# Stick-breaking attention in a two-layer decoder trunk: value products of two units placed together, projections dealt three and one per step

## The chip, the cores and the metric

The kernel runs on one core of a Trainium2 chip. The metric is the device time of one execution in microseconds; before the change the median of three runs is 2117.93 us (2116.54 to 2119.25). The engines are named as in the profile: PE multiplies matrices (PEld loads its weights, beside it), DVE is the vector engine, ACT the scalar engine, POOL the general one, and SP issues most transfers. Each engine runs its own instructions strictly in the order in which they were written, and waits on semaphores for the others.

## The reference

The model has two layers, 1024 tokens and a width of 1024, all in float32. Layer 0 is a gated linear recurrence, layer 1 stick-breaking attention with 16 heads of 64; each is followed by a SwiGLU network, and an RMS norm stands before each part and at the end. The change touches the attention alone:

```python
def stick_breaking_attention(x, w_qkv, w_o):
    qkv = jnp.einsum("bsd,de->bse", x, w_qkv).reshape(bsz, seq, 3, N_HEADS, HEAD_DIM)
    ...
    for blk in range(seq // Q_BLOCK):
        ...
        z = jnp.einsum("bhqd,bhkd->bhqk", qb, kb).astype(jnp.float32) * scale
        ...
        log_fail = jnp.where(strict, jax.nn.log_sigmoid(-z), 0.0)
        suffix = lax.cumsum(log_fail, axis=3, reverse=True) - log_fail
        weights = jnp.where(strict, jnp.exp(jax.nn.log_sigmoid(z) + suffix), 0.0)
        outs.append(jnp.einsum("bhqk,bhkd->bhqd", weights.astype(vb.dtype), vb))
```

The kernel writes the weights as differences of running products of sigmoid(-z), taken from the right. So a row of scores needs one sigmoid and one multiplying scan, and the products are taken with differences of neighbouring values (`VV`).

## The kernel before, in words

The attention stage is one loop over steps u, from -10 to 191 (line 1915), with the order of every engine written out by hand: what is written first runs first on its engine. 16 heads in 8 pairs q give 192 chunks of scores and 192 units of products, 12 of each per head, so a pair takes 24 steps. Step u does:

- the scores of chunk u + 10: two float32 matmuls into one of two PSUM buffers `z_ps` (`z_part`, lines 1690 and 1691); ACT takes their sigmoid into `w` (`z_rest`, line 1728), which frees the buffer, and DVE scans `w` (`scan`, lines 1735 and 1738);
- for the chunk of the step before, ACT casts `w` to float16 and DVE takes the remainder (`turn_weights`, lines 1750 and 1751), and a transfer on SP transposes both (line 1760);
- the products of unit u: two to four float16 matmuls into `av_ps` (`av_part`, line 1802). An even unit has them after the scan, an odd one at the end of the step. Units 3 and 11 of a head close their output bank, which ACT and DVE then gather (`oo`, lines 1814 and 1815), and POOL adds the values (line 1819);
- one task of the queue `later` (weights, norms, gathering), and at the start of the step all tasks that were staged for it (`stage` and `due`);
- from u = -2 on, two calls of the generator of projections (`fill`).

The generator (`qkv_steps`, line 1571) makes queries, keys and values of the next pair (`which` 0, 1 and 2), each in two halves n of 512 tokens. A half is eight groups of three float32 matmuls into `qk_ps` (lines 143 to 145), and each call gives one group. The eighth group ends a half and begins its eviction; the next call ends the eviction and gives the first group of the next half:

```python
                        if i < ND - 1:
                            yield
                    ev = evacuate(q, which, n, ps)
                    next(ev)
                    yield
                    next(ev, None)
```

Of an eviction (`evacuate`, line 1600) the first part reads PSUM: for queries ACT's cast `two<-qk_ps` (L1660), for keys DVE's multiplication `two<-qk_ps,rbc` (L1665), for values DVE's `vt<-qk_ps` (L1610). The second part does, for queries, DVE's low part (L1651) and stages the copies to the heads (L1648). For keys it stages ACT's cast `two<-two` (L1673) for the next step; this stages the low part (L1651) and the first two key copies (L1640) for the step after, and these the last two copies. For values it takes the difference (L1612) and stages its cast (L1627).

When the generator turns to the keys it also puts the three parts of the next weights (L1558 and L1559) and of the column norms into `later`: two squares on ACT (`sq<-raw`, L1553) and the sums on PE (`n_ps<-g,sq`, L1537). The sums take a `z_ps` buffer in turn with the scores.

For the last pair (from u = 166) the weights are transposed on PE instead (`t_part`, `t_split`, lines 1770, 1779 and 1780), two units at an even step; the generator has ended by then, and some groups of the output projection (`out_work`) fill in.

Of the kernel before, what the change touches and what calls it, by code (L numbers as in the profile page):

```python
# [34 lines left out]
def trunk(  # L35
# [166 lines left out]
    def stats(acc, ps_pool, tag, n, i0=0, i1=4):  # L202
        ps = ps_pool.tile([P, NB], F32, tag=tag, name="st_ps")
        accs = acc if isinstance(acc, tuple) else (acc,)
        for i in range(i0, i1):
            for a in accs:
                nc.tensor.matmul(
                    ps[:, i : i + 1], lhsT=a[:, i * P : (i + 1) * P], rhs=ones, start=a is accs[0], stop=a is accs[-1]
                )
        rstd(rcol[:, 4 * n + i0 : 4 * n + i1], ps[:, i0:i1])  # L210
# [1277 lines left out]
    with ExitStack() as st:  # L1488
# [31 lines left out]
        def stage(task, steps=1):  # L1520
            soon.append([steps, task])

        def load_link(i):
            q, which = divmod(i, 3)
            if q < NP:
                raws[i] = load_raw(cols(w_qkv, which * D + q * P), (ND,))
            else:
                mix[0].load(which)
# [233 lines left out]
        def unit_list(q, hx):  # L1762
            kbs = ((0, 1, 2, 3), (4, 5, 6, 7, 0, 1, 2, 3))
            return [(q, hx, G, kb, kb == 4 * G, kb == 3) for G in range(2) for kb in kbs[G]]

        def t_part(q, hx, G, kb, first, last):
            tp = psT.tile([P, NB], F32, tag="T", name="wt_ps")
            for j in range(max(kb, 4 * G), 4 * G + 4):
                c = (j - 4 * G) * P
                nc.tensor.transpose(  # L1770
                    tp[:, c : c + P], W[q, hx, j, kb // 4][:, (kb % 4) * P : (kb % 4 + 1) * P], ident
                )
            return tp
# [11 lines left out]
        def av_part(q, hx, G, kb, first, last):  # L1785
            q0 = (max(kb, 4 * G) - 4 * G) * P
            if first:
                av[0] = psO.tile([P, NB], F32, tag="o", name="av_ps")
            ps = av[0]
            k = kb % 4  # L1790
            parts_ = []
            if q == LAST:
                parts_ = [(q0, NB, t[:, q0:].rearrange("p (j c) -> p j c", c=P)) for t in ready.pop((hx, G, kb))]
            else:
                T_ = T[q, hx, G, kb // 4 == G]
                if kb // 4 == G and k < 2:
                    tp = T[q, hx, G, "pair"]
                    parts_ = [(q0, 2 * P, tp[:, x : x + 3 : 2] if k == 0 else tp[:, 4 + x : 5 + x]) for x in range(2)]
                c0 = max(q0, 2 * P) if kb // 4 == G else 0
                parts_ += [(c0, NB, T_[:, 2 * k + x, max(k - 2, 0) * (kb // 4 == G) :]) for x in range(2)]  # L1800
            for i, (c0, c1, t) in enumerate(parts_):
                nc.tensor.matmul(  # L1802
                    ps[:, c0:c1].rearrange("p (j c) -> p j c", c=P), lhsT=VV[q][:, hx, kb], rhs=t,
                    start=first and i == 0, stop=last and i == len(parts_) - 1,
                )
            if not last:
                return
            a, b = (top, bot)[:: 1 if hx == 0 else -1]

            def gather():  # L1810
                if hx == 0:
                    oo[q, G] = ap.tile([P, NB], F32, tag="oo", name="oo", bufs=2)
                o = oo[q, G]
                nc.scalar.copy(o[a], ps[b])
                nc.vector.tensor_add(o[a], ps[a], o[a])

            def add_v():
                eng = nc.vector if q == NP - 1 else nc.gpsimd
                eng.tensor_add(oo[q, G], oo[q, G], VT[q][:, G * NB + 1 : (G + 1) * NB + 1])

            def parts():
                o = oo[q, G]
                down = f32(av_[q])

                def both(hi, lo):
                    nc.scalar.activation(hi, o, AF.Copy, scale=down)
                    nc.vector.scalar_tensor_tensor(lo, o, down, f32(hi), op0=ALU.mult, op1=ALU.subtract)

                if not kept(q, G):
                    both(xh[q][G], xl[q][G])  # L1830
                else:
                    oh = ap.tile([P, NB], F32R, tag="oh", name="oh", bufs=1)
                    both(oh, o.bitcast(F32R))

                    def store():
                        nc.sync.dma_start(od[q, G][0], f32(oh))
                        nc.sync.dma_start(od[q, G][1], o)

                    stage(store)

            later.insert(0, gather)
            if hx == 1:
                later.extend((add_v, lambda: None, parts))
# [3 lines left out]
        units = [u for q, hx in heads for u in unit_list(q, hx)]  # L1847
# [27 lines left out]
        with tc.manual_schedule(engines={E.PE, E.Activation, E.DVE, E.Pool, E.SP}):  # L1875


            load_link(1)
            first = qkv_steps(0)
            between = {  # L1880
                12: lambda: stats(rbc[0], psO, "o", 0),
                16: lambda: stats(rbc[1], psO, "o", 1),
                17: lambda: broadcast_r(psO, "o", 0),
                18: lambda: nc.gpsimd.tensor_scalar_mul(rs, rcol, -SC),
                21: lambda: broadcast_r(psO, "o", 1),
            }
            def due():
                now = soon[:]
                soon.clear()
                for steps, task in now:  # L1890
                    if steps > 1:
                        stage(task, steps - 1)
                    else:
                        task()

            for i in range(1, 2 * ND * NH + 3 + AHEAD):
                next(first)
                if i in between:
                    between[i]()
                due()  # L1900
                if i > 4 and later:
                    later.pop(0)()

            gains = [len(units) - x for x in (31, 29, 27)]

            last_two, out_work = len(units) - 2 * 12, out_fill()
            amount = {x: 2 for x in (9, 10, 11, 12)}
            amount.update({x: 1 for x in (*range(-5, 1), *range(14, 21))})
            c = 0

            def turn(some):
                for a in some:
                    turn_weights(*a)

            for u in range(-LEAD, len(units)):
                some = chunks[c : c + 1]
                c += 1
                if u < -2:
                    for _ in range(2):
                        next(fill, None)  # L1920
                due()
                for _ in range(2 if u >= last_two - 8 and u % 2 == 0 else 1):
                    if back:
                        nc.sync.dma_start(*back.pop(0))
                for a in some:
                    z_rest(z_part(*a), *a)
                if u % 2 == 0 and u + 2 >= last_two:
                    av_part(*units[u])
                    two = [(x, t_part(*x)) for x in units[u + 2 : u + 4]]
                    for x, tp in two:  # L1930
                        ready[x[1:4]] = t_split(tp, *x)
                for a in some:
                    scan(*a)
                now, turning = turning, list(some)
                turn(now)
                if u % 2 == 0 and 0 <= u < last_two - 2:
                    av_part(*units[u])
                if u - last_two == 9:
                    mix[0].w[mix[0].order[1]] = next_weights(mix[0].raw.pop(1), nc.gpsimd)
                if later:  # L1940
                    later.pop(0)()
                if u >= -2:
                    for _ in range(2):
                        next(fill, None)
                for _ in range(amount.get(u - last_two, 0)):
                    next(out_work)
                if u in gains:
                    z_rest(z_part(*chunks[c]), *chunks[c])
                    scan(*chunks[c])
                    turning.append(chunks[c])  # L1950
                    c += 1
                if u % 2 and u >= 0:
                    av_part(*units[u])
            while later or soon:
                due()
                if later:
                    later.pop(0)()
# [46 lines left out]
```

## Time and profile before

| | us |
|---|---|
| median of three runs | 2117.93 |
| the profiled execution | 2116.7 |
| its span | 2114.9 |
| attention loop within the span, about | 985 to 1400 |
| PE busy | 2096.8 |
| DVE busy | 1771.3 |
| ACT busy | 1184.5 |

The span runs from the first to the last instruction; 1.8 us of the profiled execution lie outside it. Times of rows are counted from the start of the span. Matmuls are pipelined: a row's length is longer than the distance to the next row's start, and this distance is what a matmul costs. In the order of time a row has start, length, engine, line, operation, written<-read tiles and shape; idle time of the engine ahead of it stands in brackets with what ended it, and xN merges N in a row. In the list of waits a row has who waited for whom, total us, times, and the longest.

### The profile page before, as it was taken

How to read it: one execution, taken by the hardware profiler on the slowest of the kernel's cores; microseconds unless marked ns; L12 is line 12 of the kernel's file. 1: busy time of each engine (PE TensorE's matmuls, PEld its weight loads, DVE VectorE, ACT ScalarE, POOL GpSimd, SP SyncE). 2: the span in 40 equal slices, each digit the busy share in tenths (PEclk: the TensorE clock that was granted, in tenths of full speed). 3: DMA queues.
4: the chain of work that ended last, by engine and by line, in shares of the span. 5: the costliest groups of instructions: out<-in, count | busy, mean ns of one | idle time of the engine just before them, and what ended most of it. 6: DMA issues, size and time to landing. Idle time of an engine off the chain costs nothing.

```text
span 2114.9 us, 27976 instructions
## 1 busy us (share of the span) xinstructions
PE 2096.8 (99%) x10022; PEld 1719.9 (81%) x10022; DVE 1771.3 (84%) x2579; ACT 1184.5 (56%) x1906; POOL 139.1 (7%) x118
## 2 busy tenths in 40 slices
PE   8999999999999999999999999999999999999998
PEld 7888888888888888887777777678888888888887
DVE  7888778888888788796999999967888888888886
ACT  6567535444344445466878878744544444454456
POOL 1222010000000000000011111012000000000002
PEclk9999999999999999999999999999999999999999
DMA  7111431334444776533888898942224444686452
GB/s 240 50 50 40 149 100 55 105 124 145 161 133 152 256 251 190 152 118 91 162 179 175 177 178 174 247 170 80 85 90 150 140 150 155 202 269 225 126 153 90
DMA packets 446444, 313.89 MB, mean 148 GB/s; under 512 B 166104, under 2 KB 361824, under 8 KB 446304
## 3 DMA queue, kind: packets, MB, share of 16 engines
q1 hardware_dynamic: 446144, 311.84, 51.1%
q8 instruction: 78, 1.28, 0.3%
q14 instruction: 62, 0.51, 0.1%
q10 hardware_dynamic: 160, 0.27, 0.0%
HBM read 183.57 MB, written 82.84 MB: 126 GB/s over the span
## 4 chain that ended last, share of the span: by engine, by line
PE 93%; DVE 3%; ACT 1%; DMA 1%; issue 1%; SPq 0%; DVEq 0%; ACTq 0%
PE p_ps L143 18%; PE p_ps L145 18%; PE p_ps L144 18%; PE qk_ps L143 3%; PE qk_ps L145 3%; PE qk_ps L144 3%; PE a_ps L144 3%; PE a_ps L145 3%; PE a_ps L143 3%; PE ob_ps L143 3%; PE ob_ps L145 3%; PE ob_ps L144 3%; PE av_ps L1802 2%; PE i_ps L145 1%; PE i_ps L144 1%; PE i_ps L143 1%
## 5 line engine op out<-in xcount | busy, mean ns | idle before, releaser
L143 PE MATMUL p_ps<-vh,wbh 128*128 128x512 f32 x524 | 204.9, 391 | 0.0
L144 PE MATMUL p_ps<-vl,wbh 128*128 128x512 f32 x524 | 204.5, 390 | 0.0
L145 PE MATMUL p_ps<-vh,wbl 128*128 128x512 f32 x524 | 204.0, 389 | 0.2 <-DVE wbl L726 0.2
L143 PE MATMUL p_ps<-vh,wch 128*128 128x512 f32 x524 | 204.2, 390 | 0.0
L145 PE MATMUL p_ps<-vh,wcl 128*128 128x512 f32 x524 | 204.1, 389 | 0.0
L144 PE MATMUL p_ps<-vl,wch 128*128 128x512 f32 x524 | 203.9, 389 | 0.0
L722 ACT CAST wbh<-sb 128x1024 fp32r<-128x1024 f32 (+2 forms) x69 | 69.6, 1009 | 192.6 <-DVE sb L702 192.6
L145 PE MATMUL p_ps<-vh,wal 128*128 128x512 f32 x396 | 154.0, 389 | 0.0
L143 PE MATMUL p_ps<-vh,wah 128*128 128x512 f32 x396 | 154.0, 389 | 0.0
L144 PE MATMUL p_ps<-vl,wah 128*128 128x512 f32 x396 | 154.0, 389 | 0.0
L145 PEld LDWEIGHTS p_ps<-vh,wbl 128*128 128x128 f32 x524 | 98.4, 188 | 21.6 <-DVE wbl L726 0.7
L145 PEld LDWEIGHTS p_ps<-vh,wcl 128*128 128x128 f32 x524 | 98.4, 188 | 20.9 <-DVE wcl L736 0.6
L143 PEld LDWEIGHTS p_ps<-vh,wch 128*128 128x128 f32 x524 | 98.4, 188 | 20.5 <-ACT tb L1181 0.2
L144 PEld LDWEIGHTS p_ps<-vl,wch 128*128 128x128 f32 x524 | 98.3, 188 | 20.5
L143 PEld LDWEIGHTS p_ps<-vh,wbh 128*128 128x128 f32 x524 | 98.6, 188 | 19.8 <-ACT U L1181 0.4
L144 PEld LDWEIGHTS p_ps<-vl,wbh 128*128 128x128 f32 x524 | 98.6, 188 | 18.5
L143 PE MATMUL qk_ps<-vh,whi 128*128 128x512 f32 x264 | 113.2, 429 | 0.0
L1728 ACT ACTIVATE w<-z_ps,rs 128x512 f32<-128x512 f32 (+2 forms) x168 | 96.7, 579 | 15.1 <-PE z_ps L1691 12.0
L144 PE MATMUL qk_ps<-vl,whi 128*128 128x512 f32 x264 | 103.8, 393 | 0.0
L145 PE MATMUL qk_ps<-vh,wlo 128*128 128x512 f32 x264 | 103.7, 393 | 0.0
L1750 ACT CAST wx<-w 128x512 f16<-128x512 f32 (+1 forms) x140 | 80.1, 572 | 38.4 <-DVE w L1735 20.0
L1735 DVE TENSOR_TENSOR_SCAN w<-w,unit 128x128 f32<-128x128 f32 (+1 forms) x112 | 93.4, 834 | 9.5 <-ACT w L1728 8.3
(417 smaller groups left out, 5834.3 us busy)
## 6 DMA issues: line engine op xcount, KB each, us to landing
raw<-in_ffn_w_in SPq DMA_DIRECT2D x88, 512.0 KB, 4.0
vl<-pd SPq DMA_DIRECT2D x128, 256.0 KB, 3.6
pd<-U SPq DMA_DIRECT2D x90, 256.0 KB, 2.3
raw<-in_ffn_w_out SPq DMA_DIRECT2D x56, 256.0 KB, 3.6
raw<-in_attn_w_qkv SPq DMA_DIRECT2D x24, 512.0 KB, 4.2
h<-hd SPq DMA_DIRECT2D x32, 256.0 KB, 5.7
hd<-h SPq DMA_DIRECT2D x32, 256.0 KB, 2.0
g<-hd SPq DMA_DIRECT2D x32, 256.0 KB, 5.3
```

The costliest lines, as they stand in the source:

```text
L143: nc.tensor.matmul(ps, lhsT=wh, rhs=mh, start=first, stop=False, **kw)
L144: nc.tensor.matmul(ps, lhsT=wh, rhs=ml, start=False, stop=False, **kw)
L145: nc.tensor.matmul(ps, lhsT=wl, rhs=mh, start=False, stop=last, **kw)
L722: nc.scalar.copy(self.full(self.wb), self.full(self.sb))
L1728: nc.scalar.activation(F, ps[:, 0:n], AF.Sigmoid, scale=rs[:, j : j + 1])
L1735: nc.vector.tensor_tensor_scan(rev, rev, unit[:, NB - n :][:, ::-1], 0.0, op0=ALU.mult, op1=ALU.add)
L1750: nc.scalar.copy(wx[:, 0:m, 0], F)
L1802: nc.tensor.matmul(ps[:, c0:c1].rearrange("p (j c) -> p j c", c=P), lhsT=VV[q][:, hx, kb], rhs=t, start=first and i == 0, stop=last and i ...
```

## The change

Two things. The products of an even unit leave their place in the even step, in the main part and in the last pair alike, and stand at the end of the odd step, right ahead of those of the odd unit. And the generator is called three times in an even step and once in an odd one, instead of twice in each. The number of calls, of instructions and of transfers stays the same.

```diff
@@ -1925,7 +1925,6 @@
                 for a in some:
                     z_rest(z_part(*a), *a)
                 if u % 2 == 0 and u + 2 >= last_two:
-                    av_part(*units[u])
                     two = [(x, t_part(*x)) for x in units[u + 2 : u + 4]]
                     for x, tp in two:
                         ready[x[1:4]] = t_split(tp, *x)
@@ -1933,14 +1932,12 @@
                     scan(*a)
                 now, turning = turning, list(some)
                 turn(now)
-                if u % 2 == 0 and 0 <= u < last_two - 2:
-                    av_part(*units[u])
                 if u - last_two == 9:
                     mix[0].w[mix[0].order[1]] = next_weights(mix[0].raw.pop(1), nc.gpsimd)
                 if later:
                     later.pop(0)()
                 if u >= -2:
-                    for _ in range(2):
+                    for _ in range(1 if u % 2 else 3):
                         next(fill, None)
                 for _ in range(amount.get(u - last_two, 0)):
                     next(out_work)
@@ -1950,6 +1947,7 @@
                     turning.append(chunks[c])
                     c += 1
                 if u % 2 and u >= 0:
+                    av_part(*units[u - 1])
                     av_part(*units[u])
             while later or soon:
                 due()
```

## The prediction, as put on record

> **What bounds the kernel now.** I read the page's busy times and chain first, then busy time by stage, then PE's waits in the attention stage, and last the order in time of ACT, DVE and PE in one stretch of it.
>
> ```profile
> PE 2096.8 (99%) x10022; PEld 1719.9 (81%) x10022; DVE 1771.3 (84%) x2579; ACT 1184.5 (56%) x1906; POOL 139.1 (7%) x118
> PE 93%; DVE 3%; ACT 1%; DMA 1%; issue 1%; SPq 0%; DVEq 0%; ACTq 0%
> ```
>
> TensorE sets the time; every microsecond in which it waits is paid. The change touches only the attention stage, about 990 to 1400 us from the span's start. By stage (columns: PE, PEld, DVE, ACT, POOL busy, clock, DMA):
>
> ```profile
> 920.00:950.00 30.00, 30.00 (x133) 24.58 (x132) 28.16 (x50) 18.69 (x35) 0.00 (x0) 1.00 0.38 123
> 1100.00:1150.00 50.00, 50.00 (x262) 37.76 (x261) 48.16 (x69) 40.53 (x76) 5.72 (x7) 1.00 0.86 176
> 1342.00:1400.00 58.00, 54.45 (x303) 39.67 (x302) 50.69 (x74) 33.86 (x66) 5.45 (x4) 1.00 0.76 228
> ```
>
> In the middle row PE never waits, but DVE is busy 48.16 of 50 us: it has under 4% to spare, and ACT a fifth. So an edit that makes ACT and DVE wait for each other can reach PE. PE's own waits in the stage are few, all near its end:
>
> ```profile
> PE av_ps L1802 <- DVE wx L1780: 1.6, 3, 0.8
> PE ob L144 <- DMA vl<-odl: 1.1, 1, 1.1
> PE z_ps L1690 <- ACT wd L1728: 0.9, 2, 0.7
> ```
>
> **What the change moves.** Two things on PE: the value products of an even unit go one step later, and one group of three projection matmuls goes from each odd step to the even step before it. Neither adds work. But the generator of the projections also issues its evictions: with three calls in an even step, the call that ends an eight-group half (always an even step) is followed at once by the next call, which held the second half of the eviction back one step. So the second half of every eviction, and what it stages, moves one step earlier on ACT, DVE and SP. For queries it is the low part and its copies, for values the difference and its cast. For keys it is the cast `two<-two` (L1673), which reads what DVE's multiplication `two<-qk_ps,rbc` (L1665) has just written. That is where it costs. On ACT, at the first key half of the fourth head pair, before the change:
>
> ```order
> L1814 COPY oo<-av_ps 64x512 [waits DMAHW1_49]
> L1728 ACTIVATE w<-z_ps,rs 128x512 [waits PE_49]
> L1750 CAST wx<-w 128x3x128 [waits DMAHW0_49,DVE_49]
> L1558 CAST whi<-raw 128x512 [waits DMAHW4_49]
> L1673 CAST two<-two 128x512 [waits DMAHW5_49,DMAHW4_49,DVE_49]
> L1728 ACTIVATE w_10240<-z_ps,rs 128x128 [waits PE_49]
> ```
>
> and with it:
>
> ```order
> L1814 COPY oo<-av_ps 64x512 [waits DMAHW1_49]
> L1673 CAST two<-two 128x512 [waits DMAHW4_49,DMAHW3_49,DVE_49]
> L1728 ACTIVATE w<-z_ps,rs 128x512 [waits PE_49]
> L1750 CAST wx<-w 128x3x128 [waits DMAHW0_49,Activation_49]
> L1558 CAST whi<-raw 128x512
> L1640 CAST kk<-two 64x512 [waits Activation_49]
> L1640 CAST kk<-two 64x512
> L1728 ACTIVATE w_10245<-z_ps,rs 128x128 [waits PE_49]
> ```
>
> The cast passed a sigmoid, a split cast and a weight cast; the two key copies passed the next sigmoid. The cast also stands ahead of a sigmoid in the second key half, two steps on, where that sigmoid, a split cast and the second `sq` follow. On PE, the column sums `n_ps<-g,sq` that need this `sq` lose the products that stood ahead of them:
>
> ```order
> +L1802 LDWEIGHTS v
> +L1802 MATMUL av_ps<-wt,v 128x512
> +L1802 LDWEIGHTS v
> +L1802 MATMUL av_ps<-wt,v 128x512
>  L1690 MATMUL z_ps<-kk,q 128x512
>  L1691 MATMUL z_ps<-kk,q 128x512
> -L1802 LDWEIGHTS v
> -L1802 MATMUL av_ps<-wt,v 128x512
> -L1802 LDWEIGHTS v
> -L1802 MATMUL av_ps<-wt,v 128x512
>  L1537 LDWEIGHTS sq
>  L1537 MATMUL n_ps<-g_7927,sq 128x1
> ```
>
> PE now comes to the sums right after the scores.
>
> **The first key half, walked.** ACT in that stretch before the change (start, length, engine, line; in brackets the idle time and its releaser):
>
> ```profile
> 1170.66 0.58 ACT L1814 COPY oo<-av_ps 64x512 f32<-64x512 f32 x1
> 1171.28 0.69 ACT L1728 ACTIVATE w<-z_ps,rs 128x512 f32<-128x512 f32 x1
> 1171.87 0.50 ACT L1750 CAST wx<-w 128x384 f16<-128x384 f32 x1
> 1172.27 0.62 ACT L1558 CAST whi<-raw 128x512 fp32r<-128x512 f32 x1
> 1173.28 0.62 ACT L1673 CAST two<-two 128x512 fp32r<-128x512 f32 x1 [0.39 <-DVE two L1665]
> 1173.81 0.36 ACT L1728 ACTIVATE w<-z_ps,rs 128x128 f32<-128x128 f32 x1
> 1174.41 0.62 ACT L1750 CAST wx<-w 128x512 f16<-128x512 f32 x1 [0.24 <-DVE w L1735]
> 1174.94 0.61 ACT L1558 CAST whi<-raw 128x512 fp32r<-128x512 f32 x1
> 1175.46 1.24 ACT L1640 CAST kk<-two 64x512 fp32r<-64x512 f32 x2
> 1176.72 0.47 ACT L1728 ACTIVATE w<-z_ps,rs 128x256 f32<-128x256 f32 x1
> ...
> 1179.77 0.68 ACT L1728 ACTIVATE w<-z_ps,rs 128x512 f32<-128x512 f32 x1
> 1180.34 0.50 ACT L1750 CAST wx<-w 128x384 f16<-128x384 f32 x1
> 1180.74 0.63 ACT L1553 ACTIVATE sq<-raw 128x512 bf16<-128x512 f32 x1
> 1181.28 0.61 ACT L1673 CAST two<-two 128x512 fp32r<-128x512 f32 x1
> ```
>
> and DVE, which runs about a microsecond behind:
>
> ```profile
> 1170.66 0.95 DVE L1735 TENSOR_TENSOR_SCAN w<-w,unit 128x384 f32<-128x384 f32 x1
> ...
> 1172.58 0.67 DVE L1665 TENSOR_TENSOR two<-qk_ps,rbc 128x512 f32<-128x512 f32 x1
> 1173.17 1.20 DVE L1735 TENSOR_TENSOR_SCAN w<-w,unit 128x512 f32<-128x512 f32 x1
> ...
> 1177.23 0.69 DVE L1735 TENSOR_TENSOR_SCAN w<-w,unit 128x256 f32<-128x256 f32 x1 [0.28 <-ACT w L1728]
> 1177.84 0.67 DVE L1559 TENSOR_TENSOR wlo<-raw,whi 128x512 fp32r<-128x512 f32 x1
> 1178.97 0.96 DVE L1735 TENSOR_TENSOR_SCAN w<-w,unit 128x384 f32<-128x384 f32 x1 [0.47 <-ACT w L1728]
> ...
> 1180.30 0.68 DVE L1665 TENSOR_TENSOR two<-qk_ps,rbc 128x512 f32<-128x512 f32 x1
> ```
>
> The multiplication ends at 1173.25 and stands where it stood. So the cast still starts at 1173.28; what is new is that ACT, done with `oo` at 1171.24, waits 2.0 us for it with a sigmoid behind it. Starts then follow at the old rows' spacing: sigmoid 1173.81 (before 1171.28), split 1174.40, weight cast 1174.80, key copies 1175.32, next sigmoid 1176.58 (before 1173.81), ending 1176.94. The scores of two steps on need the PSUM buffer that this sigmoid frees:
>
> ```profile
> 1176.38 0.42 PE L1690 MATMUL z_ps<-kk,q 128*128 128x384 f32 x1
> ...
> 1178.65 0.39 PE L1690 MATMUL z_ps<-kk,q 128*128 128x512 f32 x1
> ...
> 1180.74 0.58 PE L1690 MATMUL z_ps<-kk,q 128*128 128x512 f32 x1
> 1181.16 0.40 PE L1691 MATMUL z_ps<-kk,q 128*128 128x512 f32 x1
> 1181.40 0.61 PE L1802 MATMUL av_ps<-wt,v 128*128 128x512 f16 x2
> 1181.84 0.34 PE L1537 MATMUL n_ps<-g,sq 128*128 128x1 bf16 x8
> ...
> 1182.36 0.39 PE L144 MATMUL qk_ps<-vl,whi 128*128 128x512 f32 x1
> 1182.59 0.40 PE L145 MATMUL qk_ps<-vh,wlo 128*128 128x512 f32 x1
> ```
>
> PE reaches it at 1176.38 and waits 0.56. The next scores come 2.27 + 3 x 0.23 - 0.44 = 2.5 us after (a group of three more, two products fewer: 1181.40 to 1181.84), at 1179.45; their buffer is freed by the sigmoid that starts 0.3 + 0.53 + 0.52 + 1.26 after 1176.58 and ends at 1179.7: 0.25 more. PE is now 0.8 late.
>
> **The second half.** That sigmoid, ended at 1179.7 instead of 1177.19, releases DVE's scan of 1177.23 at 1179.73; scan, low part, the next scan and its split (0.61, 0.60, 0.88, 0.45) bring the second multiplication to 1182.27, ending 1182.95, against 1180.98. Behind it ACT runs cast 0.53, sigmoid 0.57, split 0.40, `sq` 0.63, so the second `sq` ends at about 1185.1. PE comes to the column sums at 1181.84 - 0.44 + 0.8 = 1182.2 and waits 2.9. Together a visit costs 3.7 us. After it PE is that much later, and DVE and ACT have caught up some ten steps on, so visits don't add up.
>
> Both ends of a visit: if DVE were not late, the second multiplication ends at 1180.98, `sq` at 1183.1, and PE, there at 1181.40, waits 1.7; nothing below that is left. The upper end adds the clock. One wait in this trace shows it:
>
> ```profile
> 969.88 1.13 PE L192 MATMUL rb_ps<-ident,rcol 128*128 128x128 f32 x8 [1.91 <-DVE rcol L183]
> ...
> 972.26 0.63 PE L144 MATMUL qk_ps<-vl,whi 128*128 128x512 f32 x1
> 972.69 0.63 PE L145 MATMUL qk_ps<-vh,wlo 128*128 128x512 f32 x1
> ```
>
> After 1.91 us idle, matmuls start 0.43 us apart instead of 0.23, for some eight of them: 1.6 us lost. PE's shorter waits (up to 1.1 us) show no such stretch. A wait of 2.9 us is above the one that did it, but a single case doesn't tell whether each such wait does, so I let four visits of seven pay. The Trainium skill (TensorE: Matmul & The Clock Gate, HAM oscillation — how this bites in real kernels) has it otherwise: only PE gaps above about 3.4 us lower the clock. By that no visit would pay; the row above disagrees, with 1.91.
>
> **How many.** The loop evicts keys for seven pairs (the eighth before it). The first visit finds DVE hardly behind, so it takes the lower price: 6 x 3.7 + 1.7 = 23.9. Clock: 4 x 1.6 = 6.4.
>
> **What is gained.** An f32 matmul costs 30.00/133 = 0.226 in the pure stage before, and 0.23 here (1182.36 to 1182.59), where f16 groups stand between. The change removes one of two f16 groups per pair of steps; with 16 f32 matmuls in a pair that returns 16 x 0.004 = 0.06 us at most, nothing at least. I take half: 2.5 us over 84 pairs of steps. At the stage's end the even unit's products come a step later behind their splits, so the 1.6 us on `wx` goes. The other two waits stay: a DMA and a sigmoid set them.
>
> **What costs nothing.** The transfers that move a step earlier (queries, keys, values) pass one weight transpose each on SP; its readers come six steps, some 13 us, after. If one came late all the same, PE would wait for it at its product, at most a step of 2.3 us in a pair. Nothing waits for an even unit's product: an odd unit closes the output bank, and odd units stay at the end of their step. The query copies stood ahead of a sigmoid before too, one step later, and no scores waited for that one; the value cast moves together with the difference that it reads.
>
> **The sum.** 23.9 + 6.4 - 2.5 - 1.6 = +26.2 on the profiled run's 2116.7 us (span 2114.9), so 2142.9; the median of the runs is 1.2 above, so 2144.
>
> **Rivals.**
> 1. PE stays fed and only the gains count: 2118 - 2.5 - 1.6 = 2114, faster. It needs DVE to reach both multiplications 2 us earlier than its rows show; at 48.16 of 50 busy it can't run ahead. 0.10.
> 2. DVE's lag disappears (ACT waits, DVE catches up before the second half): 7 x 1.7 - 4.1 = +8, 2126. For it: bubbles of 0.28 and 0.47 on DVE in the stretch. 0.14.
> 3. The clock never falls, because the waits are not long enough: 23.9 - 4.1 = +20, 2138. Against it stands the one row of 1.91 us, for it that one row is all there is. 0.22. (It is what the rule of the Trainium skill named above would give.)
> 4. The lag is not worked off within a head pair (DVE's spare 4% of 50.8 us is 2 us): each later visit pays 2 us more, 2144 + 12 = 2156. 0.14.
>
> My forecast has 0.40.
>
> **Range and chances.** A difference under 0.2% (4.2 us) counts as none, about what a measurement can tell. Forecast with two to seven visits at the low clock: 2141 to 2149. With rivals 2 to 4 the range is 2120 to 2159. Rival 1 lies at the bound, so its 0.10 splits into faster 0.06 and same 0.04; of rival 2 another 0.02 may end as no change. Slower 0.88.
>
> **What would show it.** In the profile after: PE waits in the attention stage, before none until 1342, now at seven places; the longest before `n_ps`, released by ACT `sq`, about 2.9 us; shorter ones before `z_ps`, released by sigmoids; ACT's wait on L1665, at most 0.39 in the stretch shown, about 2 us; granted clock under 1.00 in the rows after. If PE shows no waits there, the walk is wrong; if waits stand elsewhere (before `av_ps` or `qk_ps`), I have the wrong queue.

## The result, and the profile after

The changed kernel takes 2149.08 us (median of 4 runs, 2145.59 to 2150.63), the kernel before 2117.23 (4 runs beside it, 2115.86 to 2119.25): a ratio of 1.0151, interval 1.0139 to 1.0163. It is slower by about 32 us; 2144 was forecast, in a range of 2120 to 2159. The profiled execution is the fastest of the four, 2145.59 us with a span of 2143.8, so 28.9 us of span have to be found.

The page's busy times and the chain of waits first:

```profile
PE 2104.6 (98%) x10022; PEld 1730.2 (81%) x10022; DVE 1769.6 (83%) x2579; ACT 1186.3 (55%) x1906; POOL 136.5 (6%) x118
PE 83%; DVE 7%; issue 5%; ACT 4%; DMA 1%; POOL 0%; DVEq 0%; SPq 0%; POOLq 0%; ACTq 0%
```

The instructions are as many as before on every engine; nothing was added. But the chain that ended last runs on PE for 83% of the span instead of 93%, and passes through DVE and ACT for 11% instead of 4%: PE is made to wait for them. Where, PE's waits in the attention stage tell (who waits, on what; us in total, times, longest):

```profile
PE n_ps L1537 <- ACT w L1728: 11.5, 7, 1.7
PE z_ps L1690 <- ACT w L1728: 5.5, 8, 0.9
PE n_ps L1537 <- ACT sq L1553: 5.0, 7, 0.8
PE wt_ps L1770 <- DVE wx L1780: 2.0, 4, 0.8
PE z_ps L1690 <- ACT wd L1728: 1.0, 1, 1.0
```

Together 25.0 us, against 3.6 before. Seven times, once per head pair whose keys the loop evicts, PE waits before the column sums `n_ps` (11.5 + 5.0 us), and some eight times before scores. The stretches of the stage read accordingly (PE, PEld, DVE, ACT, POOL busy, clock, DMA):

```profile
1100.00:1150.00 50.00, 46.73 (x243) 35.58 (x242) 44.03 (x65) 38.64 (x71) 5.48 (x7) 1.00 0.81 171
1300.00:1370.00 70.00, 64.66 (x311) 48.89 (x311) 58.30 (x84) 51.02 (x93) 5.05 (x10) 0.93 0.80 161
```

In the first, PE was busy all 50 us before and is now idle for 3.3. In the second the granted clock falls as well.

The visit that the prediction walked through, the fourth head pair, on ACT (start, length, instruction; idle time and releaser in brackets):

```profile
1180.67 0.58 ACT L1814 COPY oo<-av_ps 64x512 f32<-64x512 f32 x1
1183.29 0.62 ACT L1673 CAST two<-two 128x512 fp32r<-128x512 f32 x1 [2.04 <-DVE two L1665]
1183.94 0.69 ACT L1728 ACTIVATE w<-z_ps,rs 128x512 f32<-128x512 f32 x1
...
1185.45 1.24 ACT L1640 CAST kk<-two 64x512 fp32r<-64x512 f32 x2
1186.71 0.37 ACT L1728 ACTIVATE w<-z_ps,rs 128x128 f32<-128x128 f32 x1
...
1193.02 0.62 ACT L1673 CAST two<-two 128x512 fp32r<-128x512 f32 x1 [1.46 <-DVE two L1665]
1193.54 0.68 ACT L1728 ACTIVATE w<-z_ps,rs 128x512 f32<-128x512 f32 x1
1194.12 0.50 ACT L1750 CAST wx<-w 128x384 f16<-128x384 f32 x1
1194.52 0.63 ACT L1553 ACTIVATE sq<-raw 128x512 bf16<-128x512 f32 x1
```

and on PE:

```profile
1187.13 0.45 PE L1690 MATMUL z_ps<-kk,q 128*128 128x384 f32 x1 [0.85 <-ACT w L1728]
...
1189.43 0.39 PE L145 MATMUL qk_ps<-vh,wlo 128*128 128x512 f32 x1
1189.81 0.50 PE L1690 MATMUL z_ps<-kk,q 128*128 128x512 f32 x1
...
1192.19 0.39 PE L1691 MATMUL z_ps<-kk,q 128*128 128x512 f32 x1
1194.27 0.24 PE L1537 MATMUL n_ps<-g,sq 128*128 128x1 bf16 x4 [1.69 <-ACT w L1728]
1195.21 0.25 PE L1537 MATMUL n_ps<-g,sq 128*128 128x1 bf16 x4 [0.69 <-ACT sq L1553]
1195.32 0.47 PE L143 MATMUL qk_ps<-vh,whi 128*128 128x512 f32 x1
```

ACT stands idle for 2.04 us before the first key cast, since DVE has not yet multiplied, and for 1.46 before the second. The sigmoids behind the casts are late, and PE waits 0.85 us for scores, 1.69 and 0.69 for the column sums. The sums' first wait ends with a sigmoid, not with `sq`: line 1535 of the kernel takes `n_ps` from the pool of the scores' buffers (its tag is "z", as that of `z_ps` in line 1688), so the sums need a sigmoid to free a buffer before they need `sq`. Both stand behind the second key cast on ACT.

A bracket counts from the end of the row before (0.39 us after its start), but without a wait the next matmul starts 0.23 us after it. So the brackets give less than the waits cost. From the last scores at 1192.19 to the sums are 2.08 us: 1.85 are lost there. The second wait costs 0.83, since four sums take 0.11 (1195.21 to 1195.32) and here 0.94 pass.

DVE is held in turn. Between the two multiplications its scan of the 256-wide chunk waits for the late sigmoid:

```profile
1189.79 0.69 DVE L1735 TENSOR_TENSOR_SCAN w<-w,unit 128x256 f32<-128x256 f32 x1 [0.88 <-ACT w L1728]
...
1192.30 0.68 DVE L1665 TENSOR_TENSOR two<-qk_ps,rbc 128x512 f32<-128x512 f32 x1
```

So ACT's idle time in the first half makes DVE late, and DVE's lateness adds to ACT's idle time in the second: 1.46 us here, 1.14 in experiment 6, where the first cast is not early. The same visit one head pair earlier and later has the same waits at the sums, to 0.01 us (those before scores are 0.89 and 0.91):

```profile
1139.84 0.24 PE L1537 MATMUL n_ps<-g,sq 128*128 128x1 bf16 x4 [1.69 <-ACT w L1728]
...
1248.72 0.24 PE L1537 MATMUL n_ps<-g,sq 128*128 128x1 bf16 x4 [1.69 <-ACT w L1728]
```

From 1139.84 to 1194.27 are 54.43 us and from there to 1248.72 are 54.45. Before the change the sums came every 50.77 us, so a head pair costs 3.68 us more, and no visit makes the next one worse.

What the clock adds is to be seen at a visit near the end of the loop:

```profile
1303.17 0.24 PE L1537 MATMUL n_ps<-g,sq 128*128 128x1 bf16 x4 [1.70 <-ACT w L1728]
1304.10 0.27 PE L1537 MATMUL n_ps<-g,sq 128*128 128x1 bf16 x4 [0.69 <-ACT sq L1553]
1304.23 0.77 PE L143 MATMUL qk_ps<-vh,whi 128*128 128x512 f32 x1
1304.80 0.63 PE L144 MATMUL qk_ps<-vl,whi 128*128 128x512 f32 x1
...
1307.79 0.63 PE L145 MATMUL qk_ps<-vh,wlo 128*128 128x512 f32 x1
```

The matmuls start 0.43 us apart instead of 0.23 (1304.80 to 1307.79: seven intervals). The granted clock shows such a half-speed stretch of 6.83 us here and one of 3.41 after the next visit; the five other visits have none, though they wait as long at the sums (1.35 and 0.80 us in the first, 1.69 and 0.69 or 0.70 in the others).

The one wait from which the prediction took the clock's price, 1.91 us, comes in this profile too, 0.96 us later than before the change, and no half speed follows it:

```profile
970.84 1.13 PE L192 MATMUL rb_ps<-ident,rcol 128*128 128x128 f32 x8 [1.91 <-DVE rcol L183]
...
972.26 0.39 PE L145 MATMUL qk_ps<-xg,wlo 128*128 128x512 f32 x1
972.49 0.40 PE L143 MATMUL qk_ps<-vh,whi 128*128 128x512 f32 x1
```

So the profile before the change holds a half-speed stretch of 3.41 us, at 971, that this one lacks. PE, 0.96 us behind at the wait, reaches the first scores of the attention loop 0.64 us ahead of the kernel before. The stretch cost 1.60 us, as the prediction had it, and the loop itself adds 29.5 us, not 28.9.

### The profile page after: what moved, and what is told of

Its sections match the earlier page's. It is cut to its first block, busy times and chain, and to the rows that moved or that the text cites. A ratio compares the mean times of both kernels' runs of the same rounds, so it can differ in the third digit from the quotient of the medians.

```text
span 2143.8 us, 27991 instructions
## 1 busy us (share of the span) xinstructions
PE 2104.6 (98%) x10022; PEld 1730.2 (81%) x10022; DVE 1769.6 (83%) x2579; ACT 1186.3 (55%) x1906; POOL 136.5 (6%) x118
## 4 chain that ended last, share of the span: by engine, by line
PE 83%; DVE 7%; issue 5%; ACT 4%; DMA 1%; POOL 0%; DVEq 0%; SPq 0%; POOLq 0%; ACTq 0%
PE p_ps L143 18%; PE p_ps L145 18%; PE p_ps L144 18%; PE a_ps L144 3%; PE a_ps L145 3%; PE a_ps L143 3%; PE ob_ps L143 3%; PE ob_ps L144 3%; PE ob_ps L145 3%; DVE wx L1751 2%; PE qk_ps L143 1%; PE qk_ps L145 1%; PE qk_ps L144 1%; PE i_ps L145 1%; PE i_ps L144 1%
## 5 line engine op out<-in xcount | busy, mean ns | idle before, releaser
L143 PE MATMUL qk_ps<-vh,whi 128*128 128x512 f32 x264 | 104.9, 397 | 0.0
```

The source lines that it names most:

```text
L143: nc.tensor.matmul(ps, lhsT=wh, rhs=mh, start=first, stop=False, **kw)
```

## The experiments

The question was which part of the change costs the time: the cast that reaches ACT before its operand, or something else that the 3/1 dealing or the pairing moves. The cast had two rivals to begin with: the uneven dealing of matmuls as such, and the pairing, which takes the products from ahead of the sums. Later runs ask how the cost divides between the two key halves, and whether the sums merely come too soon. Each diff is against the changed kernel, unless "before" stands beside it. The rows are PE's waits in the attention stage.

**1. The pairing alone** (two and two again):

```diff
-                    for _ in range(1 if u % 2 else 3):
+                    for _ in range(2):
```

> The value products stand in pairs in the odd step as in the change, but the projections are dealt two per step as before. Theory (the key cast, moved a step earlier by the dealing, costs the time): no key cast moves, so PE does not wait in the middle of the attention stage; the only effect is fewer changes between f32 and f16 matmuls, about 0.3 us in 24 steps, so 2113 to 2118 us and no wait before n_ps. Rival A (the pairing costs: the column sums lose the products that covered them): waits before n_ps at seven places of 1 us and more, 2125 to 2135 us.

2118.81 us (10 runs), before 2116.36 (19 runs): 1.0010, interval 1.0001 to 1.0020 (a ratio goes by all runs and can differ from that of the medians by up to 0.0007). That is 0.8 us above the expected range. PE's waits:

```profile
PE ob L144 <- DMA vl<-odl: 2.3, 1, 2.3
...
PE n_ps L1537 <- ACT sq L1553: 0.7, 3, 0.3
```

The seven waits of 1.7 us are gone and so is all but some 2 us of the loss. The pairing does not make it, and does not gain either; the small waits at the sums were not expected. Between visits PE gets ahead of the kernel before by about 0.28 us per 24 steps, the sums' waits take about as much back, and at the stage's end the wait for the transfer `odl` is 2.3 us instead of 1.1.

**2. The dealing alone** (before, with three and one):

```diff
-                    for _ in range(2):
+                    for _ in range(1 if u % 2 else 3):
```

> The projections are dealt three and one, the products stay where they were. Theory: each visit still waits, 0.44 us less than the 4.0 us of the change because the even products stand ahead of the column sums again, and nothing is gained from the pairing: 7 x 3.5 plus 5 to 9 us of low clock, 2143 to 2152 us. Rival A (the pairing costs): 2115 to 2119 us.

2142.89 us (4 runs, 2141.97 to 2143.63), ratio 1.0120 (1.0105 to 1.0135): 0.1 us under the expected range.

```profile
PE n_ps L1537 <- ACT w L1728: 9.9, 7, 1.5
PE n_ps L1537 <- ACT sq L1553: 5.0, 7, 0.8
PE z_ps L1690 <- ACT w L1728: 3.6, 6, 0.8
```

The same waits, a little shorter, because the products still stand ahead of the sums. Most of the loss comes with the dealing. That leaves the cast, or the uneven dealing as such.

**3. The key cast held one step** (the dealing and the pairing stay; the keys' second part goes back to the step where it was):

```diff
-                stage(high)
+                stage(high, 2)
```

> The whole change, with one edit: the key cast two<-two is staged two steps ahead instead of one, so it stands in the step in which it stood before the change; queries and values stay a step early. Theory: the waits before z_ps and n_ps in the seven visits go, and the gain of the pairing is left: 2113 to 2118 us. Rival B (any of the evictions that moved, or the uneven dealing itself, costs): waits stay at part of the places, 2124 to 2145 us.

2119.64 us (10 runs, 2118.58 to 2121.11), ratio 1.0014 (1.0005 to 1.0023).

```profile
PE n_ps L1537 <- ACT sq L1553: 1.5, 5, 0.3
PE z_ps L1690 <- ACT w L1728: 0.3, 1, 0.3
```

This one edit takes back some 29 of the 32 us, with matmuls dealt three and one as in the change. So the dealing as such isn't it, nor are the second parts of queries and values, which stay early. The time is 1.6 us above the expected range: some 3 us of the loss are left, 1.5 of them in small waits at the sums. What makes the rest was not sought.

**4. The key cast one step early, and nothing else** (before; two and two, no pairing; the cast is staged before the generator gives control back, not after):

```diff
-                yield
 
                 def high():
                     nc.scalar.copy(two[:, 0], t)
                     stage(low)
 
                 stage(high)
+                yield
```

> The kernel before, with one edit: the key cast is staged a step earlier, at the end of the step of the multiplication that it reads; products and dealing are as before. Theory: this alone makes most of the loss, 7 x 3.5 us and 4 to 9 us of low clock: 2140 to 2151 us, with waits before z_ps released by ACT w and before n_ps released by ACT sq. Rival B: 2115 to 2121 us, since the dealing is as before.

2141.50 us (4 runs, 2139.67 to 2143.09), ratio 1.0113 (1.0096 to 1.0130).

```profile
PE n_ps L1537 <- ACT w L1728: 6.1, 7, 1.0
PE n_ps L1537 <- ACT sq L1553: 4.5, 7, 0.7
PE z_ps L1690 <- ACT w L1728: 2.7, 10, 0.5
```

Putting the cast early in a kernel that is otherwise the one before costs 24 us by the ratio, 25 by the medians. With experiment 3 the cause stands from both sides: taking it out of the change removes all but some 3 us of the loss, and it alone makes three quarters of it. The waits are shorter than in the change, but in four of seven visits half speed follows waits of about 1.0 and 0.7 us.

**5. The dealing shifted by one call** (one call fewer at u = -3, so that a half ends on another call of its step):

```diff
-                    for _ in range(2):
+                    for _ in range(1 if u == -3 else 2):
```

> The whole change, with one call of the generator fewer in step -3, so that all later calls shift by one: the eighth group of a half is then the third and last call of its even step, and the second half of each eviction falls in the next step again, for queries, keys and values alike. Theory: same as holding the key cast alone: the waits go, 2115 to 2121 us, with at most some tenths of a microsecond before n_ps in a visit, as the two kernels that paired the products without the early cast had it. Rival B (the uneven dealing itself bunches the work of ACT and DVE): 2124 to 2145 us.

2119.09 us (10 runs), before 2116.69 (21 runs): 1.0008 (0.9999 to 1.0017). PE's wait at the sums:

```profile
PE n_ps L1537 <- ACT sq L1553: 2.4, 7, 0.5
```

Three and one do no harm where the call that ends a half is the last of its step. So it is not three groups in a row that cost, but what the next call issues right behind the eighth.

**6. The first key cast held, the second early:**

```diff
-                stage(high)
+                stage(high, 2 - n)
```

> The whole change, with the key cast of the first half (n = 0) held in its old step and that of the second half left a step early. The prediction's walk gives each its price: without the first early cast DVE is not late at the second multiplication, the waits before z_ps go and that before n_ps falls from 2.4 to about 1.7 us: 2119 + 7 x 1.7 = 2131 us, less low clock than in the change (0 to 3 us more). Rival C (the two act independently, the first making only its own 1.3 us before z_ps): 7 x 2.7 us are left, 2138 to 2144 us.

2133.00 us (4 runs, 2132.37 to 2133.37), ratio 1.0072 (1.0058 to 1.0086).

```profile
PE n_ps L1537 <- ACT w L1728: 6.1, 6, 1.3
PE n_ps L1537 <- ACT sq L1553: 4.9, 7, 0.8
PE z_ps L1690 <- ACT w L1728: 0.9, 2, 0.7
```

The waits for scores nearly go. The sums come every 52.45 us in visits without low clock, so the second cast alone costs 1.68 us per visit, net of what the pairing returns (0.28, experiment 1), where the walk gave 1.7 with DVE not late. Visits with a half-speed stretch take 53.72, so a stretch of 3.41 us costs about 1.3 net: PE comes later to the next sums and waits 0.76 us there instead of 1.07. The rival's 2138 to 2144 did not come.

**7. The second key cast held, the first early:**

```diff
-                stage(high)
+                stage(high, 1 + n)
```

> The whole change, with the key cast of the second half (n = 1) held in its old step and that of the first half left a step early. By the walk the waits before z_ps stay, 0.8 to 1.3 us a visit, and the column sums wait little, since no cast stands ahead of the sigmoid and the second square: 2119 + 7 x 1.2 = 2127 us (2124 to 2131), with the clock at 1.00. Rival C: the first early cast costs nothing that lasts, 2117 to 2121 us.

2133.53 us (4 runs, 2131.52 to 2134.13), ratio 1.0073 (1.0060 to 1.0087). This missed its expectation by 2.5 us beyond its upper end.

```profile
PE z_ps L1690 <- ACT w L1728: 4.9, 7, 0.9
PE n_ps L1537 <- ACT sq L1553: 3.5, 7, 0.8
PE n_ps L1537 <- ACT w L1728: 1.4, 1, 1.4
```

The first cast alone costs 2.16 us per visit (52.93 between sums, again net), not the 0.8 of its score waits: the lateness that it leaves on ACT and DVE still holds the second `sq` back by half a microsecond on average. The two casts are about equally dear, and their prices nearly add: 16.1 us come back by holding the first, 15.6 the second, 29.4 by holding both.

**8. The pairing with the sums moved behind the first projections** (before; in even steps `later`'s task stands between the two calls, the even unit's products go to the odd step):

```diff
-                if u % 2 == 0 and 0 <= u < last_two - 2:
-                    av_part(*units[u])
...
+                if u % 2 == 0 and u >= -2:
+                    next(fill, None)
                 if later:
                     later.pop(0)()
                 if u >= -2:
-                    for _ in range(2):
+                    for _ in range(1 + u % 2):
                         next(fill, None)
...
                 if u % 2 and u >= 0:
+                    if u < last_two - 2:
+                        av_part(*units[u - 1])
                     av_part(*units[u])
```

> A try at keeping the gain alone: projections two per step, products paired in the main part but not in the last pair (there as before the change), and in even steps the task of later, the column sums among them, stands between the two projection groups instead of ahead of both. Theory: pairing gains 0.28 us in 24 steps, as the trace of the pairing alone shows it between the column sums; with three matmuls as new cover the sums no longer wait, and the last pair loses nothing: 2 us under the kernel before, 2113.5 to 2116 us. Rival D: moving the task displaces ACT's or DVE's work and a new wait appears, 2117 us or more.

2118.61 us (11 runs, 2114.70 to 2121.58), ratio 1.0002 (0.9993 to 1.0011): a miss, no gain. The sums never wait, and in the middle of the loop PE is up to 1.1 us ahead of the kernel before, by the starts of its scores. But 0.47 us of that it has before the loop begins, since this profile has no half speed behind the wait of 1.91 us. It enters the last pair 0.62 ahead and leaves it 0.2 behind. The transfer `odl` lands when it did (PE goes on at 1356.50, before at 1356.53), so PE arriving earlier only waits longer: 2.3 us, 1.1 before.

**9. The sums one step later, in the changed kernel** (a task that does nothing stands ahead of them in `later`; the factors that follow are staged one step nearer):

```diff
-                stage(factors, 2)
+                stage(factors)
...
-            return lambda: squared(0), lambda: squared(1), sums
+            return lambda: squared(0), lambda: squared(1), lambda: None, sums
```

> The whole change, with the column sums one step later (a task that does nothing ahead of them) and their factors staged one step instead of two, so that the values find them in time. The sums then come 2.5 us later on PE, when the second square is done. Theory: ACT is behind by that much, not only the square, so the wait moves rather than goes: the sums now need the buffer that the next sigmoid but one frees, which by the trace of the change ends 1.8 us after the second square; 2.0 to 2.7 us a visit stay before n_ps or z_ps, released by ACT w, and the time is 2140 to 2149 us. Rival E (only the square was late): the 2.7 us before n_ps go, 1.3 us a visit before z_ps stay, 2124 to 2132 us.

2145.36 us (4 runs, 2143.56 to 2145.87), ratio 1.0136 (1.0121 to 1.0152). PE's waits, and then the visit of above in PE's order of time:

```profile
PE n_ps L1537 <- ACT w L1728: 13.7, 7, 2.1
PE z_ps L1690 <- ACT w L1728: 7.1, 12, 0.9
```

```profile
1195.56 0.39 PE L1691 MATMUL z_ps<-kk,q 128*128 128x512 f32 x1
1197.88 0.34 PE L1537 MATMUL n_ps<-g,sq 128*128 128x1 bf16 x8 [1.93 <-ACT w L1728]
```

The sums come a step later and no longer wait for `sq`; behind the scores of 1195.56 PE waits 1.93 us all the same, for a sigmoid. The wait moves, it does not go (20.8 us before sums and scores together, 22.0 in the change): ACT's queue is late, not the sums early. The rival (2124 to 2132) falls.

**10. The pairing left out where it costs** (before; an even unit keeps its own step in the steps of the sums and in the last pair):

```diff
+            alone = lambda u: u == 8 or u % 24 == 10
...
-                if u % 2 == 0 and 0 <= u < last_two - 2:
+                if u % 2 == 0 and 0 <= u < last_two - 2 and alone(u):
                     av_part(*units[u])
...
                 if u % 2 and u >= 0:
+                    if u < last_two - 2 and not alone(u - 1):
+                        av_part(*units[u - 1])
                     av_part(*units[u])
```

> The kernel before, with the products paired in the main part except in the steps of the column sums, and not in the last pair; two projections per step. Theory: in the trace PE runs ahead of the kernel before by 0.25 us in each 24 steps, 1.5 to 2 us at the start of the last pair, with no wait before n_ps; but the last pair is held by transfers and by DVE (busy 22.91 of 23 us there), so PE waits that much longer and the time stays within 2115 to 2118 us. Rival F (the gain is kept): 2113 to 2115 us.

2117.13 us (11 runs, 2113.78 to 2119.27), ratio 0.9998 (0.9990 to 1.0007). No wait above 0.1 us is left in the loop. In this profile PE reaches the loop 0.85 us behind the kernel before and the last pair level with it, so the loop gains 0.84 us where 1.5 to 2 were expected; 0.69 of that come in the first three pairs, and why the gain then stops is open. PE leaves the last pair 1.1 us behind, with the wait for `odl` at 2.3 us again.

None of the ten beats the kernel before by more than its interval.

## Why the prediction was right

**The mechanism** is as forecast: the second key part comes a step early, ACT idles for DVE's multiplication, and the sigmoids and `sq` behind it make PE wait. The walk had 2.0 us of idle time before the first cast; it is 2.04. It had waits for scores of 0.56 + 0.25; the first is 0.85, and the second, which no bracket shows, some 0.15 (the scores start at 1189.81, and the projection before them at 1189.43, where 0.23 is the usual distance). It had 2.9 us at the sums; by their brackets they are 1.69 + 0.69 = 2.38, by the distances of starts 1.85 + 0.83 = 2.68. Experiments 3 and 4 show the cast as the cause, 6 and 7 its two halves.

**The price of a visit** was 3.7 us, and it is 3.68 between sums. That agreement is partly luck. The 3.68 are net of the pairing's return, which the prediction booked apart; gross it is near 4.0. The sums' wait was 0.2 shorter than walked, and the waits for scores were longer.

**The releaser at the sums** was named too simply. The prediction waited for `sq` alone; the longer part ends with the sigmoid that frees the scores' buffer. Experiment 9 shows that this is a wait of its own: with `sq` long done, it is still 1.93 us. Both stand behind the same cast, so the sum did not suffer. By these rows an earlier `sq` alone could at most have saved the shorter part; no run tried it.

**The first visit** was put at 1.7, because DVE would not be late yet. It cost 3.1 (scores 0.7 us ahead of the kernel before when it begins, 2.4 behind when it is over), nearly as much as the others. The sums of this visit do not stand where the walk had them. They come at 1023.77, between the two key casts (1019.92 and 1029.76), so the first cast alone, with 1.97 us of idle time, holds them. Experiment 7, which has only that cast early, shows the same waits there (1.36 and 0.80 us for 1.35 and 0.80), experiment 6 only 0.76.

**Visits don't add up**: 54.43 and 54.45 us in a row. Rival 4 (lag carried over) falls, and with it 2156.

**The clock** was four visits at 1.6 us, 6.4 in all; the four was a guess between none and seven. In the profiled run it is three stretches of 3.41 us after two visits, 3.9 at the 1.3 of experiment 6. The other three runs show a granted clock of 0.994 and 0.995 instead of 0.997 and spans that are 3.4 to 5.0 us longer. If the whole of that is clock, the median run paid about 7 us for it, and the size was right there. Rival 3 (no low clock) falls. But the single case behind the price was no rule: the same wait of 1.91 us comes without half speed in the profile of the change. The Trainium skill (TensorE: Matmul & The Clock Gate, HAM oscillation — how this bites in real kernels) gives as its rule that PE should have no idle gaps above about 3.4 us; the trace disagrees in so far as the stretch at 1304 follows two waits of 1.70 and 0.69 us.

**The gains** did not come. This is the step that failed. Pairing does return what was taken for it, about 0.28 us per 24 steps, or 0.023 per pair of steps where 0.03 was taken. But in experiments 1, 8 and 10, where no early cast is in the way, the kernel's time shows none of it. Part is lost inside the loop already: by the starts of the scores, PE gains nothing between the loop's begin and the last pair in experiment 1, 0.15 us in 8 and 0.84 in 10. The last pair takes the rest. The 1.6 us at the stage's end did not come either: the waits of `av_ps` on `wx` are gone, and transposes now wait for the splits in their place.

```profile
L1802 PE MATMUL av_ps<-wx,v x48: 219/352/390, 1391.8 to 1423.3; 128*128 128x512 f16 x24, 128*128 128x384 f16 x8, 128*128 128x256 f16 x8, 128*128 128x128 f16 x8
```

That is the last pair's products (min, median and max ns, first and last start). In the kernel before they ran until 1394.3; the last starts 28.9 us later, which is the whole difference of the spans. PE came into the last pair 28.9 late as well, so the pair returned nothing. The wait was put on the products' place in the order, but it hangs on DVE, which has no room there before the change:

```profile
1342.00:1365.00 23.00, 21.07 (x116) 15.13 (x115) 22.91 (x33) 14.02 (x28) 1.09 (x1) 1.00 1.05 264
```

DVE is busy 22.91 of 23.00 us. Whoever reaches it earlier waits longer. That this, with the transfer `odl`, is what swallows the rest of the pairing's gain in experiments 8 and 10 is argued from these rows; no run relieved DVE or the transfer in the last pair to show it.

**The account** of the profiled run: PE's waits +21.4 (25.0 less 3.6), low clock +3.9, together 25.3 of the loop's 29.5. The other 4.2 are what the brackets leave out, less the pairing's return; they were not counted row by row. The forecast's 26.2 is 3.3 below these 29.5. With the visits taken at their net 3.68, gains of 4.1 that did not come and 1.4 more at the first visit, against 2.5 less clock, leave 0.3 that nothing explains. The span grew by 28.9 only, since PE reached the loop 0.64 ahead. The median lies 5 us above the forecast, at the upper end of the 2141 to 2149 that it had for two to seven visits at low clock; by their granted clock the other runs spent longer at half speed, but where is not known.

## What to carry to other kernels

When a change moves the calls of a generator, ask what each call issues besides the work that it is named for: here a group of matmuls moved, and the cast behind it cost 24 us by itself. On an engine that runs in order, an instruction that comes before its operand can cost more than its own wait (2.16 us per visit on PE for 2.04 of idle time on ACT in experiment 7, 1.68 for 1.14 in experiment 6): walk the queue behind it to the next buffer that must come free, and look up which tiles share that buffer. A gain on the engine that sets the time is kept only if the stage's last part is set by that engine too; where another engine or a transfer ends it, time gained ahead may be spent waiting, as the rows of the last pair suggest here.

## What the hardware showed that was not expected

Half speed followed two waits close to each other although neither was long: 1.70 and 0.69 us at 1304 in the changed kernel, where the granted clock falls at 1303.6, and about 1.0 and 0.7 in experiment 4, in four of seven visits. Equal waits had it after some visits and not after others: two of seven here, two in experiment 2, three in 6, none in 7, two in 9. The same holds of a single wait. The one at 970, 1.91 to 1.93 us long, stands in all twelve profiles, and half speed follows it in eight, but not in those of the changed kernel and of experiments 4, 8 and 9. What decides is open. The stretches last 3.41 us, or twice that; one cost 1.6 us behind the wait at 970 and about 1.3 net in the loop.
